# One hybrid trunk layer on one core: the last gate goes to memory in one write by rows, and the writes of the turned residual stand further apart

## The chip, the core and the metric

The kernel runs on one core of a Trainium2 chip. The metric is the device time of one execution in microseconds (us), start to end; lower is better. The core's engines work side by side, each through its own list of instructions in a fixed order: TensorE (PE in the profile; PEld is its loading of weights), VectorE (DVE), ScalarE (ACT), GpSimd (POOL) and SyncE (SP). A DMA is issued by one of them, stands in that engine's list, and is carried out beside it.

## What is computed

One layer over 128 context tokens and 256 latent tokens, 2048 wide, in single precision. Six modulation vectors come from `c` (latent) and `c_ctx` (context). The sixth, `g2`, is the last gate: it weighs the output of the feed-forward part before the residual is added.

```python
m = (jax.nn.silu(cvec) @ w_ada + b_ada)          # adaln: 6 x 2048, for c_ctx and for c
sh1, sc1, g1, sh2, sc2, g2 = split(m, 6)
h = rmsnorm(x, norm_mix) * (1.0 + sc1) + sh1
x = x + g1 * token_mixers(h)                     # w_in, four mixers, w_out
h = rmsnorm(x, norm_ffn) * (1.0 + sc2) + sh2
a = dwconv3(h @ w_up, w_conv)                    # 2048 -> 2 x 5632
val, gate = split(a, 2)
x = x + g2 * ((val * silu(gate)) @ w_down)       # 5632 -> 2048
y = rmsnorm(x, norm_final)
```

## The kernel before

**Tiling.** Until the feed-forward part, activations lie with features on the 128 partitions: `x2` is four tiles of 4 x 384 (four blocks of 128 features, 384 tokens). Every product is done three times, with high and low parts of both factors: each weight chunk of 128 x 1024 (512 KB, tile `raw`) is loaded by SP, cast to `whi` on ACT (line 90 of the profile is the helper that records all DVE and ACT work), and the rest `wlo` is taken on DVE. Chunks are loaded into five `raw` buffers, so SP issues a load when DVE and ACT are done with an older one.

**Feed-forward part.** The 44 blocks of hidden features are cut into three parts of 16, 14 and 14 (`PARTS`). Each part is an up-projection (`up_group`: two blocks at a time, eight chunks of `w_up`, 24 matmuls of 384 tokens per chunk into five rotating accumulators) and then a down-projection (`down_group`: four quarters `q4` of the 2048 outputs, matmuls of 512 columns) whose output has tokens on the partitions. Only the last part's down-projection adds the gate and the residual (`base`, `collect`). For that both must be had with tokens on partitions, and they go through memory:

- `turn` (spawned in the second group of the first part) transposes each `x2[q4]` on DVE in blocks of 32 x 32 into a tile `turn` and writes that to `turned` with 16 DMAs of 32 x 12 x 32 elements, issued by POOL.
- `ada_mod_dve(5, ...)` makes the gate `g2`. Its 32 weight chunks (`w_ada_dve`, through the same `raw` buffers) are mixed among the up-projection's chunks of the first part; DVE multiplies and adds them into two rows `aacc`. After each eighth chunk, that is for each quarter, a `later` sums the partitions with 16 small matmuls (`ps_mod`), transposes on DVE (`tr`), adds the bias into `mods` (features on partitions), and then calls `out`, which writes the quarter's `mods[:, 5]` to `gates` with two DMAs on POOL, one per token group, element by element: 128 x 4 single values each.
- `base(q4)` reads `gates` back, broadcast over the partitions, and `turned`.

**Order.** Nothing is scheduled by the hardware. A planner (`Pipe`) walks the chunks in order, keeps an estimated time `now`, and lets generators ("threads") emit their next piece when their time has come: `yield 12.0` means that the generator continues 12 us of planner time later. The result is one fixed list per engine. At run time an instruction waits only for the one ahead of it on its engine and for data and buffers; a planned pause is no wait.

Of the kernel before, what the change touches and what calls it, by code (L numbers as in the profile page):

```python
# [7 lines left out]
F32 = mybir.dt.float32  # L8
# [6 lines left out]
P = 128  # L15
D = 2048
KD = D // P
# [217 lines left out]
def trunk(ctx, tc, a, o):  # L235
# [6 lines left out]
    tmp = ctx.enter_context(tc.tile_pool(name="tmp", bufs=2))  # L242
# [19 lines left out]
    pipe = Pipe(nc, {"spare": Spare(), "pairs": Pairs(), "raw": WPool(5), "hi": WPool(3), "lo": WPool(3)}, {"raw": 5, "pairs": 4}, 2, 2.5)  # L262
    V, S, G, PE, SY = pipe.V, pipe.S, nc.gpsimd, nc.tensor, nc.sync

    def slot(name, dtype=F32, shape=(P, 4, T)):
        return sp.tile(list(shape), dtype, tag="s", name=name)
# [4 lines left out]
    def wide(name):  # L271
        return hp.tile([P, 512], F32, name=name, tag="v2", bufs=4)
# [10 lines left out]
    def misc(name):  # L283
        return psm.tile([P, 512], F32, tag="m", name=name)
# [24 lines left out]
    ident = misc_c[:, 0:P]  # L309
# [20 lines left out]
    mods = const.tile([P, 6, KD, 2], F32, name="mods")  # L330

    gates = dram.tile([2, D], F32, name="gates")
# [109 lines left out]
    def columns(ps, n, place):  # L442

        tr = tmp.tile([P, 8, 32], F32, name="tr")
        V.transpose(tr[:, 0:n].rearrange("p j c -> p (j c)"), ps[:, 0:32 * n])
        j0 = 0
        for i, k0, m in place:
            dst = mods[:, i, k0:k0 + m]
            V.tensor_add(dst, tr[:, j0:j0 + m, 0:2], b_ada[:, i, k0:k0 + m].unsqueeze(2).to_broadcast([P, m, 2]))
            if i in (1, 4):  # L450
                nm = at["norm_mix" if i == 1 else "norm_ffn"][:, k0:k0 + m]
                V.scalar_tensor_tensor(out=dst, in0=dst, scalar=1.0, in1=nm.unsqueeze(2).to_broadcast([P, m, 2]), op0=ALU.add, op1=ALU.mult)
            j0 += m
# [29 lines left out]
    ada_acc, pending, ada_done = {}, [], {}  # L483

    def ada_dve(src, key, k2, place, then=None):

        def mm(c):
            raw = c["raw"].rearrange("p (k n) -> p k n", k=2)
            if k2 == 0:
                while len(pending) > 1:  # L490
                    pipe.finish(pending.pop(0))
                ada_acc[key] = [wide("aacc0"), wide("aacc1")]
            t = ada_acc[key]
            for kk in range(2):
                k = 2 * k2 + kk
                for v in range(2):
                    if k == 0:
                        V.tensor_scalar(out=t[v], in0=raw[:, kk], scalar1=sv[:, k, v:v + 1], scalar2=None, op0=ALU.mult)
                    else:
                        V.scalar_tensor_tensor(out=t[v], in0=raw[:, kk], scalar=sv[:, k, v:v + 1], in1=t[v], op0=ALU.mult, op1=ALU.add)  # L500
            if k2 == 7:
                def later():
                    ps = misc("ps_mod")
                    for v in range(2):
                        for s in range(4):
                            PE.matmul(ps[32 * s:32 * s + 32, 0:P], pick[:, 31 - v:63 - v], t[v][:, s * P:(s + 1) * P], start=v == 0, stop=v == 1, tile_position=(0, 32 * s))
                    pipe.now += 0.56
                    yield 0.4
                    columns(ps, 4, place)
                    yield  # L510
                    if then:
                        then()
                pending.append(later())
                ada_done[key] = pending[-1]
                pipe.spawn(pending[-1], "d")
            yield 0.0
        return dict(src=src, mm=mm, split=False)

    def ada_mod_dve(i, q4s):
        def out(q4):  # L520
            for v in range(2):
                G.dma_start(gates[v].rearrange("(m p) -> p m", p=P)[:, 4 * q4:4 * q4 + 4], mods[:, i, 4 * q4:4 * q4 + 4, v])
        return [ada_dve(a["w_ada_dve"][i - 2, q4, k2], (i, q4), k2, [(i, 4 * q4, 4)], (lambda q4=q4: out(q4)) if i == 5 else None)
                for q4 in q4s for k2 in range(8)]


# [429 lines left out]
    for g in range(N_WIN):  # L956
        if g == W_CB:
            before = len(last)
        last += win_group(g, 2, evs.get(g) or (lambda zt, m, t, hd=g - W_H0: ev_head(zt, m, t, hd)))
    side_dve = [c for i, q4s in ADA_DVE if i == 2 for c in ada_mod_dve(i, q4s)]  # L960
    side_pe = [c for i, hs in ADA_PE for c in ada_mod_pe(i, hs)]
    side_pe, held = side_pe[:-len(ADA_HELD)], side_pe[-len(ADA_HELD):]
# [150 lines left out]
    def turn():  # L1113

        for q4 in range(4):
            t = slot("turn").rearrange("p k t -> p (k t)")
            V.transpose(t, x2[q4].rearrange("p k t -> p (k t)"))
            yield "d"
            for i in range(4):
                for q in range(4):  # L1120
                    f = (4 * q4 + i) * P + 32 * q
                    G.dma_start(turned.rearrange("(b i) f -> i b f", i=32)[:, :, f:f + 32], t[32 * q:32 * q + 32, i * T:(i + 1) * T].rearrange("p (b j) -> p b j", j=32))
            yield 12.0

    def g_slots(i):
        gh[i] = slot(f"gh{i}", F32R)
# [2 lines left out]
    def up_group(part, i):  # L1129
# [3 lines left out]
        for k2 in range(8):  # L1133
            def pre(k2=k2):
                if k2 == 0 and i == 0:
                    if part == 0:
                        pipe.finish(FF["norm"])
                    gh.clear()
                    gl.clear()
                if k2 == 0 and i % 2 == 0:  # L1140
                    g_slots(i // 2)
                if k2 == 0 and i == 1 and part == 0:
                    pipe.spawn(turn())
                if part == 0 and i == 0:
                    need_h(min(2 * k2 + 4, KD))

            def mm(c, k2=k2):
                if k2 == 0:
                    accs.extend([acc("acc0"), None, acc("acc2"), None])
                    accs[1], accs[3] = acc("acc1"), acc("acc3")  # L1150
                hi = c["hi"].rearrange("p (k n) -> p k n", k=2)
                lo = c["lo"].rearrange("p (k n) -> p k n", k=2)
                for m in (0, 2, 1, 3):
                    w = slice(m * P, (m + 1) * P)
                    for kk in range(2):
                        k = 2 * k2 + kk
                        mm_a(accs[m][:, 0:T], hi[:, kk, w], lo[:, kk, w], hh[k // 4][:, k % 4], hl[k // 4][:, k % 4], k == 0, k == KD - 1)
                        yield 3 * T_MM
                    if k2 == 7 and m >= 2:
                        pipe.start(glu(accs[m - 2][:, 0:T], accs[m][:, 0:T], b0 + m - 2, kb + m - 2))  # L1160
            out.append(dict(src=a["w_up"][b0 // 2, k2], mm=mm, pre=pre))
# [28 lines left out]

    def base(q4):

        pipe.finish(ada_done[5, q4])
        f = slice(512 * q4, 512 * q4 + 512)
        rows[q4], gate[q4] = slot(f"rows{q4}"), slot(f"gate{q4}")
        rows[q4] = rows[q4].rearrange("p k t -> p (k t)").rearrange("p (g f) -> p g f", g=NG)
        gate[q4] = gate[q4].rearrange("p k t -> p (k t)").rearrange("p (g f) -> p g f", g=NG)
        G.dma_start(gate[q4][:, 0:2], gates[:, f].rearrange("(o v) f -> o v f", o=1).to_broadcast([P, 2, 512]))
        G.dma_start(rows[q4], turned[:, f].rearrange("(g p) f -> p g f", p=P))
        G.dma_start(gate[q4][:, 2], a["norm_row"][f].rearrange("(o f) -> o f", o=1).to_broadcast([P, 512]))  # L1200
        yield 9.0
        for g in range(NG):
            V.tensor_mul(sums[q4][:, g], sums[q4][:, g], gate[q4][:, min(g, 1)])
            V.tensor_add(sums[q4][:, g], sums[q4][:, g], rows[q4][:, g])
            yield
# [40 lines left out]
    def down_group(part, q4):  # L1246
# [30 lines left out]
        return out  # L1277

    g2 = [c for i, q4s in ADA_DVE if i == 5 for c in ada_mod_dve(i, q4s)]
    for part, (b0, n) in enumerate(PARTS):  # L1280
        ups = [c for i in range(n // 2) for c in up_group(part, i)]
# [132 lines left out]
```

## Time and profile before

| | |
|---|---|
| median of 3 runs | 1787.3 us |
| the runs | 1788.08, 1778.97, 1787.3 us |
| the profiled execution's own time | 1780.96 us |
| span in its trace (first to last instruction) | 1779.2 us |
| TensorE busy | 1741.4 us, 98% |
| DVE, ACT, POOL busy | 1120.3, 711.3, 72.6 us |
| mean granted TensorE clock | 0.994 of full speed |

The trace counts time from the start of the span; 1.8 us of the profiled execution lie around it. In rows of stretches, PE is the time in which a matmul was under way, with the count of matmuls in brackets, and PEclk the granted clock. The first up-projection runs from about 657 to 945 us, its down-projection follows.

### The profile page before, as it was taken

Reading aid. Unit: us, or ns where it says so; the run is one execution under the profiler, and the core shown is the slowest. Engines: PE = TensorE matmul, PEld = TensorE weight load, DVE = VectorE, ACT = ScalarE, POOL = GpSimd, SP = SyncE. Lnnn points to the kernel's source line nnn. Section 1 sums busy time; section 2 is a strip of 40 time slices with the busy share of each in tenths; the row PEclk is TensorE's granted clock in tenths of the full one; section 3 lists DMA queues with packets and bytes.
Section 4 is the critical chain, followed back from the end, with each engine's and each line's share of the span. In section 5 each row is a group of like instructions: output and inputs, shape, how many; then the busy total and the mean of one; then the engine's idle time right before and its main releaser. Section 6 shows DMA issues by size and latency. Waiting matters only on the chain.

```text
span 1779.2 us, 26710 instructions
## 1 busy us (share of the span) xinstructions
PE 1741.4 (98%) x10704; PEld 1613.7 (91%) x10704; DVE 1120.3 (63%) x1871; ACT 711.3 (40%) x1074; POOL 72.6 (4%) x118
## 2 busy tenths in 40 slices
PE   8999999999999999998999999999999999999998
PEld 6989889989989989997998889999998899999886
DVE  4595678888986578886975333545543344464656
ACT  5523342234643256343433323434432233443433
POOL 0000000000001002500000000000000000000000
PEclk9999999999999999999999999999999999999999
DMA  8878776576645755776677344443443354434642
GB/s 336 283 286 307 278 255 227 184 245 215 218 131 179 294 209 171 244 189 154 204 164 160 127 128 129 130 126 123 131 127 127 125 166 130 125 125 135 221 140 97
DMA packets 93246, 326.69 MB, mean 184 GB/s; under 512 B 11393, under 2 KB 13697, under 8 KB 93121
## 3 DMA queue, kind: packets, MB, share of 16 engines
q1 hardware_dynamic: 86640, 307.78, 53.8%
q0 software_dynamic: 5760, 16.01, 3.0%
q8 instruction: 84, 1.38, 0.3%
q10 hardware_dynamic: 720, 1.18, 0.2%
q14 instruction: 42, 0.34, 0.0%
HBM read 318.10 MB, written 6.83 MB: 183 GB/s over the span
## 4 chain that ended last, share of the span: by engine, by line
PE 61%; DVE 4%; DMA 4%; ACT 1%; issue 1%; POOL 0%; ACTq 0%; DVEq 0%; POOLq 0%
PE acc L530 13%; PE acc L528 13%; PE acc L529 13%; PE acc L535 7%; PE acc L534 7%; PE acc L533 7%; DMA raw<-in_w_up 4%; DVE aacc L90 1%; DVE wlo L90 1%; DVE glu L90 1%; PE ps_sc L287 0%; DMA xr<-in_xT 0%; ACT whi L90 0%; PE ps_ada L468 0%; DVE xr L90 0%
## 5 line engine op out<-in xcount | busy, mean ns | idle before, releaser
L90 DVE TENSOR_TENSOR wlo<-raw,whi 128x1024 fp32r<-128x1024 f32 x384 | 468.8, 1222 | 502.5 <-ACT whi L90 500.4
L90 ACT CAST whi<-raw 128x1024 fp32r<-128x1024 f32 x384 | 402.9, 1050 | 879.7 <-PE acc L529 380.2
L528 PE MATMUL acc<-h2h,whi 128*128 128x384 f32 x1408 | 473.4, 336 | 9.5 <-ACT whi L90 5.7
L530 PE MATMUL acc<-h2h,wlo 128*128 128x384 f32 x1408 | 472.9, 336 | 2.4 <-DVE wlo L90 2.4
L529 PE MATMUL acc<-h2l,whi 128*128 128x384 f32 x1408 | 472.3, 335 | 0.3
L528 PEld LDWEIGHTS acc<-h2h,whi 128*128 128x128 f32 x1408 | 265.8, 189 | 12.5 <-ACT whi L90 6.7
L530 PEld LDWEIGHTS acc<-h2h,wlo 128*128 128x128 f32 x1408 | 265.7, 189 | 4.3 <-DVE wlo L90 4.3
L529 PEld LDWEIGHTS acc<-h2l,whi 128*128 128x128 f32 x1408 | 265.7, 189 | 0.9 <-DVE h2l L90 0.8
L535 PE MATMUL acc<-whi,gl 128*128 128x512 f32 x528 | 205.5, 389 | 0.0
L534 PE MATMUL acc<-wlo,gh 128*128 128x512 f32 x528 | 205.4, 389 | 0.0
L533 PE MATMUL acc<-whi,gh 128*128 128x512 f32 x528 | 205.4, 389 | 0.0
L528 PE MATMUL acc<-hh,whi 128*128 128x384 f32 x576 | 199.2, 346 | 0.9 <-DVE z L90 0.9
L530 PE MATMUL acc<-hh,wlo 128*128 128x384 f32 x576 | 193.2, 336 | 0.8 <-DVE wlo L90 0.8
L529 PE MATMUL acc<-hl,whi 128*128 128x384 f32 x576 | 192.8, 335 | 0.2 <-DVE hl L90 0.2
L90 DVE SCALAR_TENSOR_TENSOR aacc<-raw,svp,aacc 128x512 f32<-128x512 f32 x270 | 184.7, 744 | 0.0
L90 DVE SCALAR_TENSOR_TENSOR glu<-up,sm,glu 128x127 f32<-128x127 f32 (+1 forms) x352 | 135.3, 414 | 26.7 <-ACT glu L90 20.5
L528 PEld LDWEIGHTS acc<-hh,whi 128*128 128x128 f32 x576 | 108.1, 188 | 11.8 <-issue 7.5
L534 PEld LDWEIGHTS acc<-wlo,gh 128*128 128x128 f32 x528 | 99.1, 188 | 20.7
L535 PEld LDWEIGHTS acc<-whi,gl 128*128 128x128 f32 x528 | 99.1, 188 | 20.5
L533 PEld LDWEIGHTS acc<-whi,gh 128*128 128x128 f32 x528 | 99.1, 188 | 20.4
L530 PEld LDWEIGHTS acc<-hh,wlo 128*128 128x128 f32 x576 | 108.1, 188 | 1.5 <-DVE wlo L90 1.5
L529 PEld LDWEIGHTS acc<-hl,whi 128*128 128x128 f32 x576 | 108.2, 188 | 1.0 <-DVE hl L90 0.4
(175 smaller groups left out, 1610.1 us busy)
## 6 DMA issues: line engine op xcount, KB each, us to landing
raw<-in_w_up SPq DMA_DIRECT2D x176, 512.0 KB, 3.6
raw<-in_w_in SPq DMA_DIRECT2D x88, 512.0 KB, 4.8
raw<-in_w_down SPq DMA_DIRECT2D x88, 512.0 KB, 3.5
raw<-in_w_ada SPq DMA_DIRECT2D x64, 512.0 KB, 5.6
raw<-in_w_ada_dve SPq DMA_DIRECT2D x64, 512.0 KB, 4.5
raw<-in_w_ada_pe SPq DMA_DIRECT2D x64, 512.0 KB, 4.9
raw<-in_w_out SPq DMA_DIRECT2D x32, 512.0 KB, 4.3
x<-in_xT SPq DMA_DIRECT2D x4, 768.0 KB, 7.9
```

Of the source, the lines that this page charges most:

```text
L90: return f(*args, **kw)
L528: PE.matmul(out, wh, xh, start=first, stop=False)
L529: PE.matmul(out, wh, xl, start=False, stop=False)
L530: PE.matmul(out, wl, xh, start=False, stop=last)
L533: PE.matmul(out, xh, wh, start=first, stop=False)
L534: PE.matmul(out, xh, wl, start=False, stop=False)
L535: PE.matmul(out, xl, wh, start=False, stop=last)
```

## The change

The write of the gate is made once, after the last quarter, in place of two writes after each. DVE gathers `mods[:, 5]` into `gate_v` (128 x 32, token group by token group), one transpose on TensorE turns it into 32 rows of 128 (`ps_gate`), ACT copies them out of the accumulator memory (`gate_r`), and one DMA on POOL writes 32 runs of 128 elements. `base` no longer waits in the planner for the gate's quarter; that the write has been emitted is asserted. In `turn` the pause now stands inside the loop over the four blocks, after every fourth write, and is 14 in place of 12.

```diff
+    def rows_of_gate():
+        g = tmp.tile([P, 2, KD], F32, name="gate_v", bufs=1)
+        V.tensor_copy(g, mods[:, 5].rearrange("p m v -> p v m"))
+        yield
+        ps = misc("ps_gate")
+        PE.transpose(ps[0:2 * KD, 0:P], g.rearrange("p v m -> p (v m)"), ident)
+        yield 0.3
+        t = tmp.tile([2 * KD, P], F32, name="gate_r", bufs=1)
+        S.copy(t, ps[0:2 * KD, 0:P])
+        G.dma_start(gates.rearrange("v (m p) -> (v m) p", p=P), t)
+        gate_out.append(1)
...
     def ada_mod_dve(i, q4s):
-        def out(q4):
-            for v in range(2):
-                G.dma_start(gates[v].rearrange("(m p) -> p m", p=P)[:, 4 * q4:4 * q4 + 4], mods[:, i, 4 * q4:4 * q4 + 4, v])
-        return [ada_dve(..., (lambda q4=q4: out(q4)) if i == 5 else None)
+        def out():
+            pipe.spawn(rows_of_gate())
+        return [ada_dve(..., out if (i, q4) == (5, 3) else None)
...
                     G.dma_start(turned.rearrange(...)[:, :, f:f + 32], t[32 * q:32 * q + 32, i * T:(i + 1) * T]...)
-            yield 12.0
+                yield 14.0
...
     def base(q4):
-        pipe.finish(ada_done[5, q4])
+        assert gate_out
```

POOL's list from the second normalisation's small power (`n_q`) to the first read of the last part, before:

```order
L385 TENSOR_TENSOR n_q<-n_r,mhalf 128x3
L1122 DMA turned<-turn 32x12x32 x64
L522 DMA gates<-mods 128x4x1 x8
L1198 DMA gate_14632<-gates 128x2x512
L1199 DMA rows_14631<-turned 128x3x512
```

and with the change:

```order
L385 TENSOR_TENSOR n_q<-n_r,mhalf 128x3
L1136 DMA turned<-turn 32x12x32 x60
L529 DMA gates<-gate_r 32x128
L1136 DMA turned<-turn 32x12x32 x4
L1212 DMA gate_14631<-gates 128x2x512
L1213 DMA rows_14630<-turned 128x3x512
```

Eight writes of the gate have become one; it stands ahead of the last four writes of `turned`, and nothing else stands between the writes of `turned`.

DVE's list around the gate's first quarter (`tr` and `mods`; `turn` is the block transpose of one residual tile `xr`), before:

```order
L90 STREAM_TRANSPOSE turn<-xr_5907 128x1536
L90 TENSOR_TENSOR wlo<-raw,whi 128x1024 x2
L90 SCALAR_TENSOR_TENSOR aacc_7000<-raw,svp,aacc_7000 128x512
L90 SCALAR_TENSOR_TENSOR aacc_7001<-raw,svp,aacc_7001 128x512
L90 SCALAR_TENSOR_TENSOR aacc_7000<-raw,svp,aacc_7000 128x512
L90 SCALAR_TENSOR_TENSOR aacc_7001<-raw,svp,aacc_7001 128x512
L90 TENSOR_TENSOR wlo<-raw,whi 128x1024
L90 STREAM_TRANSPOSE tr<-ps_mod 128x128
L90 TENSOR_TENSOR mods<-tr,sm 128x8
L90 TENSOR_TENSOR wlo<-raw,whi 128x1024
```

and with the change:

```order
L90 TENSOR_TENSOR wlo<-raw,whi 128x1024
L90 STREAM_TRANSPOSE tr<-ps_mod 128x128
L90 TENSOR_TENSOR mods<-tr,sm 128x8
L90 STREAM_TRANSPOSE turn<-xr_5166 128x1536
L90 TENSOR_TENSOR wlo<-raw,whi 128x1024
```

Before, the fourth residual tile (`xr_5907`) is turned ahead of the gate's first quarter; now the second one (`xr_5166`) is turned right behind it. Counted in weight splits (`wlo`) from the kernel's start, the four block transposes stood behind the 130th, 134th, 138th and 142nd and now stand behind the 130th, 145th, 160th and 176th; the gate's four quarters stand behind the 145th, 159th, 173rd and 185th in both.

TensorE's list around the new transpose, with the change:

```order
L542 MATMUL acc_8858<-h2h_6713,whi 128x384
L543 MATMUL acc_8858<-h2l_6714,whi 128x384
L544 MATMUL acc_8858<-h2h_6713,wlo 128x384
L542 MATMUL acc_8858<-h2h_6713,whi 128x384
L543 MATMUL acc_8858<-h2l_6714,whi 128x384
L544 MATMUL acc_8858<-h2h_6713,wlo 128x384
L525 MATMUL ps_gate<-misc_c,gate_v 32x128
L542 MATMUL acc_8859<-h2h_6713,whi 128x384
L543 MATMUL acc_8859<-h2l_6714,whi 128x384
```

Six more matmuls of the up-projection stand ahead of these, so twelve in all between the gate's last small products (`ps_mod`) and the transpose (`ps_gate`); before, the same row of matmuls runs on without it.

## Rows read from the trace of the kernel before

**Rows 1.** The page's first part: busy us, share of the span, instructions.

```profile
PE 1741.4 (98%) x10704; PEld 1613.7 (91%) x10704; DVE 1120.3 (63%) x1871; ACT 711.3 (40%) x1074; POOL 72.6 (4%) x118
```

**Rows 2.** Engines by stretches: us; busy (count) of PE, PEld, DVE, ACT, POOL; PEclk; DMA; GB/s.

```profile
692.86:751.00 58.14, 58.14 (x338) 58.14 (x337) 55.40 (x84) 22.30 (x30) 33.48 (x55) 1.00 0.72 224
757.60:776.00 18.40, 17.75 (x100) 16.82 (x99) 14.72 (x28) 5.79 (x9) 1.57 (x3) 1.00 0.86 137
776.00:810.00 34.00, 33.71 (x195) 33.40 (x194) 32.60 (x53) 15.51 (x22) 0.00 (x0) 1.00 0.65 215
812.00:846.00 34.00, 27.04 (x143) 25.76 (x142) 19.60 (x35) 10.11 (x16) 1.54 (x2) 0.90 0.72 139
...
884.00:912.00 28.00, 24.21 (x122) 23.57 (x121) 15.80 (x23) 7.30 (x11) 1.49 (x2) 0.88 0.88 156
912.00:939.00 27.00, 27.00 (x157) 27.00 (x156) 26.44 (x44) 10.46 (x14) 0.00 (x0) 1.00 0.64 214
941.00:960.00 19.00, 19.00 (x91) 16.47 (x91) 13.71 (x25) 10.97 (x17) 1.47 (x2) 1.00 0.89 81
```

**Rows 3.** The chain that ended last, in order of time: start us, us, what.

```profile
760.76 12.40 DMA raw<-in_w_up
...
816.29 17.77 DMA raw<-in_w_up
...
887.28 14.75 DMA raw<-in_w_up
...
939.52 0.57 PE ps_mod L506 x16
```

**Rows 4.** DMA issues of 692 to 757.6, then of 886 to 903: KB, us to landing.

```profile
raw<-in_w_up SPq DMA_DIRECT2D x15, 512.0 KB, 4.9
...
raw<-in_w_up SPq DMA_DIRECT2D x2, 512.0 KB, 14.5
```

**Rows 5.** POOL's instructions in order of time: start us, us, what, idle before.

```profile
692.86 7.37 POOL L1122 DMA_DIRECT2D turned<-turn  x12 [42.38 <-DVE glu L90]
...
757.64 1.52 POOL L522 DMA_DIRECT2D gates<-mods  x2
...
814.44 1.54 POOL L522 DMA_DIRECT2D gates<-mods  x2 [55.27 <-DVE mods L90]
...
886.41 1.49 POOL L522 DMA_DIRECT2D gates<-mods  x2 [70.43 <-DVE mods L90]
...
940.97 1.49 POOL L522 DMA_DIRECT2D gates<-mods  x2 [53.07 <-DVE mods L90]
```

**Rows 6.** DMA issues of the whole span: KB each, median us to landing.

```profile
turned<-turn POOLq DMA_DIRECT2D x64, 48.0 KB, 4.4
...
gates<-mods POOLq DMA_DIRECT2D x8, 2.0 KB, 15.6
```

**Rows 7.** TensorE's matmuls in order of time, behind the second pair of gate writes.

```profile
826.93 0.34 PE L530 MATMUL acc<-h2h,wlo 128*128 128x384 f32 x1
829.86 0.45 PE L528 MATMUL acc<-h2h,whi 128*128 128x384 f32 x1 [2.59 <-ACT whi L90]
...
835.64 0.69 PE L528 MATMUL acc<-h2h,whi 128*128 128x384 f32 x1 [3.56 <-ACT up L90]
836.13 0.52 PE L529 MATMUL acc<-h2l,whi 128*128 128x384 f32 x1
```

**Rows 8.** DVE's instructions in order of time: a block transpose, and the last quarter.

```profile
744.79 1.77 DVE L90 STREAM_TRANSPOSE turn<-xr 128x1536 f32<-128x1536 f32 x1
...
940.51 0.17 DVE L90 TENSOR_TENSOR mods<-tr,sm 128x8 f32<-128x8 f32 x1
942.28 1.22 DVE L90 TENSOR_TENSOR wlo<-raw,whi 128x1024 fp32r<-128x1024 f32 x1 [1.60 <-ACT whi L90]
```

**Rows 9.** Four transposes on TensorE in the mixers, and ACT's copy of their output.

```profile
518.73 0.60 PE L835 MATMUL ps_vt<-misc_c,hw 128*128 128x128 f32 x4
...
519.37 0.59 ACT L90 COPY vT<-ps_vt 128x512 f32<-128x512 f32 x1 [2.70 <-PE ps_vt L835]
```

More of the change, by code (lines that the diff above doesn't have):

```diff
@@ L517, in ada_dve @@
         return dict(src=src, mm=mm, split=False)
+    def rows_of_gate():
[9 more added lines that the diff above has]
+        gate_out.append(1)
+    gate_out = []
     def ada_mod_dve(i, q4s):
-        def out(q4):
-            for v in range(2):
-                G.dma_start(gates[v].rearrange("(m p) -> p m", p=P)[:, 4 * q4:4 * q4 + 4], mods[:, i, 4 * q4:4 * q4 + 4, v])
-        return [ada_dve(a["w_ada_dve"][i - 2, q4, k2], (i, q4), k2, [(i, 4 * q4, 4)], (lambda q4=q4: out(q4)) if i == 5 else None)
+        def out():
+            pipe.spawn(rows_of_gate())
+        return [ada_dve(a["w_ada_dve"][i - 2, q4, k2], (i, q4), k2, [(i, 4 * q4, 4)], out if (i, q4) == (5, 3) else None)
                 for q4 in q4s for k2 in range(8)]
```

## The prediction, made before the changed kernel ran

> **What bounds the kernel now.** I read the page's first part, then the chain of waits in order of time, then engines by stretches around the place that the diff touches, then the transfers there. TensorE is busy 1741.4 of 1779.2 us [rows 1], so only time that it loses can be won. The diff touches the first up-projection, 657 to 945 us. There the chain, elsewhere a string of matmuls, three times passes through a weight load that is far too long: 12.40 us from 760.76, 17.77 from 816.29, 14.75 from 887.28 [rows 3]; over the stretch 692 to 757.6 the same 512 KB take 4.9 us [rows 4]. Each of the three starts 1 to 3 us behind a pair of gate writes on POOL's queue (757.64, 814.44, 886.41; the fourth pair at 940.97) [rows 5]. Such a write carries 2 KB in 512 single elements and takes 15.6 us to land; a write of a turned tile carries 48 KB and takes 4.4 [rows 6]. While a pair is under way the core's traffic falls from 224 GB/s to 137, 139, 156 and 81 [rows 2], and 512 KB loads take 14.5 us in the third such stretch [rows 4]. The fourth pair is the best witness: at 941 the gate's own products on DVE are over and the down-projection runs, yet traffic falls all the same, and TensorE, with loads ready ahead, loses nothing (19.00 busy of 19.00).
>
> What TensorE loses is more than its idle time. At 829.86 it had waited 2.59 us, at 835.64 another 3.56, and it then restarts at the lower of its two clock levels: one matmul takes 0.52 us where one takes 0.34 us otherwise [rows 7]; the granted clock is 0.90 over 812 to 846 and 0.88 over 884 to 912 [rows 2]. So I count matmuls, which takes in both. The undisturbed pace is 58.14 us / 338 = 0.172 us, and 27.00 / 157 = 0.172 again [rows 2].
>
> **What the change removes.** Lost time is stretch minus count times pace [rows 2]; no small products for the gate fall into these stretches:
> 757.6 to 776: 18.40 - 100 x 0.172 = 1.20
> 776 to 810 (the tail of the first): 34.00 - 195 x 0.172 = 0.46
> 812 to 846: 34.00 - 143 x 0.172 = 9.40
> 884 to 912: 28.00 - 122 x 0.172 = 7.02
> 941 to 960: 0.
> Sum 18.1 us, the bound of this part's gain. All 4096 single elements go; one write of 32 rows of 128 elements stands in for them. It issues where the fourth pair did (about 943 us), where even 81 GB/s cost nothing, and its reader comes only in the last down-projection. I price it at 0; its upper end is the 1.2 us of the first pair.
>
> **What it adds.** A copy of 32 columns on DVE: DVE idles 1.60 us between the last gate addition (940.51, 0.17 us) and the next split at 942.28 [rows 8], and a copy of this size costs about what the addition did. The transpose on TensorE is on the path. Four transposes with four times the weight columns took 0.60 us together [rows 9], so one is between 0.15 and 0.60; I take 0.2. It stands 12 matmuls, 2.1 us, behind the gate's products, which end near 940.1 (939.52 + 0.57) [rows 3]; what it waits for is ready near 940.9. That is 1.2 us of slack; if DVE were later than that, every up-matmul behind the transpose would wait as long. The copy out on ACT stands ahead of the accumulators' copies and costs at most 0.59 (a copy of 512 columns) [rows 9]; five accumulator buffers cover it, without them it is on the path.
>
> **What it moves.** The four big transposes on DVE keep their 1.77 us each [rows 8], and so does the first one its place. The next three move by 11, 22 and 34 weight splits: to right behind the gate's addition of the first quarter, one split behind that of the second and three behind that of the third. Their writes follow, and here the diff's longer pause says more than the program does: POOL's queue holds nothing between the 16 writes of one tile, so the pause spaces tiles, not writes. A tile's writes still leave in one burst, as the 12 that went in 7.37 us from 692.86 [rows 5]. Only the last four are apart, behind the gate's write, which waits for ACT; nobody waits for them before the last part. So three bursts come to stand almost where the three harmful gate writes stood. What a burst costs is read from 692.86 to 757.6, where all four ran: through 751 TensorE is busy 58.14 of 58.14 and 224 GB/s flow beside DVE's 55.40 [rows 2]. I take 0 us; the far end is what a harmful pair cost, 9.4 each. DVE has less idle time left when the stalls are gone: it is at 55.40 of 58.14 with four transposes inside and at 26.44 of 27.00 later, without TensorE waiting [rows 2]. I take 0 for that too.
>
> A rule that speaks against the first of these zeros: the Trainium skill, "DMA: Bandwidth & Descriptors", Specifications, wants at least 512 B in one run and has shorter ones handled by read-modify-write. A burst is 16 x 384 runs of 128 B, six times the 1024 elements of a gate pair, so counted by short runs a burst would be the worse of the two, and the sum would be rival A's, 1791, not 1763. The trace does not bear that out: 224 GB/s with bursts, 137 to 156 with gate writes.
>
> The sum: 1780.96 - 18.1 + 0.2 = 1763.1 us for the profiled execution. It is 6.3 under the median; the four known executions lie at 1779, 1781, 1787 and 1788. One trace can't tell where the other 8 us sit. The stalls differ from pair to pair within one run (1.7, 9.4, 7.0, 0), so part of the spread may be theirs and go with them (1763), or it is elsewhere and stays (1769). **I forecast 1765 us.**
>
> **Rivals.**
> A, slower: the bursts take over. They now meet the stretches with the shallowest lead, where weight loads and the gate's own loads share five buffers. If a burst holds loads back as a gate pair does, three cost, at the worst pair's price, 3 x 9.4 = 28.2: 1780.96 - 18.1 + 28.2 = 1791, and 1797 against the median. It decides near 12 us from issue to landing: the load of 12.40 us cost 1.7 in all, those of 17.77 and 14.75 cost 9.4 and 7.0 [rows 3]. Against it: in the stretch with all four bursts loads landed in 4.9 us [rows 4].
> B, part stays: one burst or the fuller DVE queue costs about 9, half of the gain: 1772, or 1778 against the median. For it: DVE at 26.44 of 27.00 [rows 2].
> C, the gate writes are not the cause: the loads of the gate's weights, or the boundary between its quarters, stall the queue, and the time stays 1781 to 1787. Against it: the fourth pair, where those loads are over and 81 GB/s remain, and the undisturbed 912 to 939 where they run at 214 GB/s [rows 2]. By the Trainium skill, "DMA: Bandwidth & Descriptors", Anatomy of one DMA, a transfer costs a constant 2.0 us plus its bytes, and many descriptors can be emitted before it shows; by that rule 2 KB writes would harm nobody and C would hold with no change in time. The trace disagrees, with 15.6 us to landing for 2 KB.
>
> **How the numbers follow.** Forecast 0.73, A 0.05, B 0.14, C 0.08. The measurement tells about 0.5% from no change, which is 8.9 us: faster means under 1778.4, slower over 1796.2. The forecast is faster throughout, B mostly, C and most of A are neither: faster 0.84, same 0.12, slower 0.04. Low end: the fastest run less the sum is 1778.97 - 18.1 = 1760.9, and I allow 4 more for a second spread that goes with the stalls: 1757. High end: B against the median, 1778, which leaves out A and C and a little of B.
>
> **What would show it.** In the new profile: no single-element writes; traffic near 200 GB/s and a granted clock of 1.00 over the whole up-projection up to its end, which comes some 18 us sooner; no wait of the weights' cast for a load beyond 5 us; three bursts of turned writes near 755, 815 and 885 us with TensorE busy beside them; the new transpose without idle time ahead of it. It is wrong if TensorE idles over 1 us behind a burst (A, B), if long loads remain without gate writes (C), or if the transpose waits for DVE.

## The result and the profile after

The changed kernel takes 1762.8 us (median of four runs, 1761.6 to 1763.6), the kernel before 1786.1 in runs beside it (1779.0 to 1788.1). The ratio is 0.9876, 95% interval 0.9847 to 0.9905: faster by 1.2%. The forecast was 1765 within 1757 to 1778. The profiled execution took 1763.55 us with a span of 1761.8, against 1780.96 and 1779.2.

The page's first part, same columns as [rows 1]:

```profile
PE 1734.2 (98%) x10705; PEld 1609.6 (91%) x10705; DVE 1120.8 (64%) x1872; ACT 713.3 (40%) x1075; POOL 67.1 (4%) x111
```

TensorE does one instruction more (the transpose) and is busy 7.2 us less, though its work has not shrunk: fewer of its matmuls ran at the lower clock. The other 10 us of the gain are idle time.

Engines by stretches, kernel after; the first six lines are the stretches of [rows 2] up to 912 us (846 to 882 has been added), the last one holds the new end of the up-projection:

```profile
692.86:751.00 58.14, 58.14 (x337) 58.14 (x336) 52.65 (x84) 23.66 (x32) 9.88 (x16) 1.00 0.65 204
757.60:776.00 18.40, 18.40 (x108) 18.40 (x107) 17.89 (x34) 8.14 (x13) 8.02 (x14) 1.00 0.72 211
776.00:810.00 34.00, 33.97 (x203) 33.54 (x201) 30.65 (x50) 15.54 (x22) 0.00 (x0) 1.00 0.63 201
812.00:846.00 34.00, 34.00 (x198) 34.00 (x197) 31.47 (x51) 14.15 (x20) 9.72 (x16) 1.00 0.75 233
846.00:882.00 36.00, 36.00 (x221) 35.55 (x220) 31.80 (x52) 14.84 (x21) 0.00 (x0) 1.00 0.64 203
884.00:912.00 28.00, 28.00 (x163) 28.00 (x163) 27.25 (x44) 12.78 (x19) 7.30 (x12) 1.00 0.65 203
924.00:942.00 18.00, 18.00 (x87) 15.46 (x86) 13.14 (x25) 10.73 (x18) 2.96 (x5) 1.00 0.47 143
```

Read four columns. PE is busy throughout. From 757 to 846 us 509 matmuls run in the three stretches where 438 ran (8 of the 509 are small products of the gate, which stood outside these stretches before), and 163 in 884 to 912 where 122 ran. The granted clock is 1.00 everywhere (it was 0.90 and 0.88). The traffic stays between 203 and 233 GB/s in the stretches that fell to 137, 139 and 156. POOL's count shows where the turned tiles' writes now are: 14, 16 and 12 of them in just these stretches.

What ACT's cast of the weights waited for, from 690 us to the end of the gate's quarters (in total, times, longest). Before:

```profile
ACT whi L90 <- DMA raw<-in_w_up: 97.5, 26, 13.0
```

After:

```profile
ACT whi L90 <- DMA raw<-in_w_up: 45.4, 18, 4.7
```

The long waits are gone (longest 4.7 in place of 13.0 us). The chain that ended last goes through one load of the up-projection's weights, of normal length, where [rows 3] had three of 12 to 18 us. The after kernel's chain in order of time (start, us, what) begins the stage with the first line and ends it with the third:

```profile
658.51 0.44 PE acc L543
...
805.52 3.62 DMA raw<-in_w_up
...
921.94 0.57 PE ps_mod L506 x16
```

The same first matmul in the chain of before:

```profile
657.25 0.45 PE acc L529
```

From the first up-matmul to the gate's last small products it takes 939.52 - 657.25 = 282.27 us before [rows 3] and 921.94 - 658.51 = 263.43 after: 18.8 less. Ahead of it the after kernel happens to be 1.26 us later, in code that the change leaves alone. Behind it 1779.2 - 939.52 = 839.7 us before and 1761.8 - 921.94 = 839.9 after, 0.2 more. So the whole gain of the span, 17.4 us, is in this stage.

### The profile page after: what moved, and what is told of

Same layout as the page of the kernel before. It is cut to its first block, busy times and chain, and to the rows that moved or that the text cites. A ratio compares the mean times of both kernels' runs of the same rounds, so it can differ in the third digit from the quotient of the medians.

```text
span 1761.8 us, 26700 instructions
## 1 busy us (share of the span) xinstructions
PE 1734.2 (98%) x10705; PEld 1609.6 (91%) x10705; DVE 1120.8 (64%) x1872; ACT 713.3 (40%) x1075; POOL 67.1 (4%) x111
## 4 chain that ended last, share of the span: by engine, by line
PE 68%; DVE 2%; DMA 1%; ACT 0%; issue 0%; POOL 0%; DVEq 0%; POOLq 0%
PE acc L542 15%; PE acc L544 15%; PE acc L543 15%; PE acc L549 7%; PE acc L547 7%; PE acc L548 7%; DMA xr<-in_xT 0%; PE ps_sc L287 0%; PE ps_ada L468 0%; DVE glu L90 0%; DVE aacc L90 0%; DVE wlo L90 0%; DVE xr L90 0%; DMA raw<-in_w_up 0%; PE ps_bc L287 0%
```

## The experiments

Each kernel was timed beside the kernel before on the same chip. In the three sets of runs, the kernel before had medians of 1791.4, 1783.8 and 1794.0 us, so each ratio goes by its own neighbour. The times that were expected were set by the 1786 us of the first runs; on the slower chips the kernels that keep the price can come out above them, as the kernel before does.

### Which part of the change is it?

The write of the gate alone: the after kernel with the old pause, which puts the turned tiles' writes back to their early place.

```diff
-                yield 14.0
+            yield 12.0
```

> The changed kernel with the old pause: one write of the gate by rows, the turned tiles' writes bunched between 692 and 758 us as before. Theory (the single-element writes alone held the loads back; the pause brings nothing): 1763 us, ratio to before 0.987, TensorE not idle through the whole up-projection, and within 2 us of the changed kernel. Rival (the pause is part of the gain, since the first gate pair met the fourth tile's burst): 1765 us or more, with the lost time behind 757 us. Rival (another cause at the gate's quarters): 1786 us.

Measured 1762.2 us (1761.5 to 1763.0), ratio 0.984 [0.9818, 0.9862]. Two stretches of it:

```profile
692.00:757.00 65.00, 65.00 (x389) 64.56 (x388) 59.62 (x90) 25.76 (x36) 38.10 (x63) 1.00 0.74 231
757.60:776.00 18.40, 18.40 (x108) 18.40 (x107) 18.15 (x34) 7.87 (x12) 0.39 (x1) 1.00 0.62 179
```

63 of the 64 turned writes stand in 65 us again, beside a TensorE that is busy in all of them, and none stands in the next two stalls' places. The gain is whole without the pause.

The pause alone, in the kernel before:

```diff
-            yield 12.0
+                yield 14.0
```

> The kernel before with the new pause alone: four gate pairs of single elements stay, three bursts of turned writes now stand right behind them on POOL's queue. Theory: none of the gain, 1783 to 1788 us; a burst behind a gate pair waits in POOL's list or adds a little, so up to 1792. Rival (the pause gives part of the gain): under 1780 us. Three long loads of 12 us and more remain behind the gate pairs in the theory.

Measured 1793.6 us (1790.0 to 1796.8), ratio 1.0014 [0.9996, 1.0031]. Its chain in order of time holds the three long loads as before:

```profile
758.31 18.87 DMA raw<-in_w_up
...
825.57 19.36 DMA raw<-in_w_up
...
898.43 17.88 DMA raw<-in_w_up
```

So the pause is worth nothing, and the gate's write is the whole change.

### What about the gate's write is dear?

The after kernel differs from before in the number of writes, their place in time, and their form. The next kernels keep number and place (two writes behind each quarter, on POOL) and alter the form alone. The first writes runs of four elements (16 B), contiguous on both sides; the gate then lies in memory in another order, and the last part reads it as if it lay in the old one. So this kernel and the next four (all up to the one with fewer single elements) compute another output; their times show what the writes cost beside the same loads and the same matmuls.

```diff
-                G.dma_start(gates[v].rearrange("(m p) -> p m", p=P)[:, 4 * q4:4 * q4 + 4], mods[:, i, 4 * q4:4 * q4 + 4, v])
+                d = gates.rearrange("v f -> (v f)").rearrange("(q p m v) -> p q m v", p=P, q=4, v=2)[:, q4]
+                G.dma_start(d[:, 2 * v:2 * v + 2].rearrange("p m v -> p (m v)"), mods[:, i, 4 * q4 + 2 * v:4 * q4 + 2 * v + 2].rearrange("p m v -> p (m v)"))
```

> The kernel before with its eight gate writes in their places and of the same 2 KB each, but as 128 runs of 16 bytes in place of 512 of 4 (the gate's values land in another order in memory, which the last part then reads so). Theory (the price goes by the number of runs): a pair is under way about 4 us in place of 13 to 16, no load lasts over 9 us, TensorE loses under 2 us in all, 1763 to 1766 us. Rival (the price goes by the write, its place or its bytes): 1786 us, with the same three long loads.

Measured 1763.0 us (1762.7 to 1763.2), ratio 0.9844 [0.9822, 0.9866]: all of the gain, with the same 2 KB per write, the same issuer and the same places behind the quarters. DMA issues (count, KB each, median us to landing):

```profile
gates<-mods POOLq DMA_DIRECT2D x8, 2.0 KB, 3.8
```

The second puts the four elements of a partition side by side in memory, where they stood 512 B apart. A whole write fills one piece of 2 KB there in both kernels; only the order within it changes. In `mods` the four stay every second element, so each is still a run of its own on that side.

```diff
-                G.dma_start(gates[v].rearrange("(m p) -> p m", p=P)[:, 4 * q4:4 * q4 + 4], mods[:, i, 4 * q4:4 * q4 + 4, v])
+                G.dma_start(gates[v].rearrange("(q p m) -> p q m", p=P, q=4)[:, q4], mods[:, i, 4 * q4:4 * q4 + 4, v])
```

> The kernel before with its eight gate writes as single elements still, 512 of them each, but landing side by side in memory (runs of four neighbours, each written on its own, in another order than the last part expects) in place of 512 bytes apart. Theory (the number of runs counts, not where they land): the stalls stay, 1783 to 1788 us, gate writes land after 12 to 17 us. Rival (scattered targets in memory are the price): the writes land within 6 us and the time is 1763 to 1770 us.

Measured 1798.4 us (1795.3 to 1803.3), ratio 1.0042 [1.0023, 1.006]: no better, rather a little worse. Its writes:

```profile
gates<-mods POOLq DMA_DIRECT2D x8, 2.0 KB, 17.0
```

The two kernels write to neighbouring places alike; they differ in whether a partition's four elements are read as one run or as four. But a write of runs also has a quarter of the runs. So the next one has 512 runs of 16 B in each write, as many as there were single elements, by sending each partition's run four times (the line removed is the same as above, here and in the next two):

```diff
+                d = gates.rearrange("v f -> (v f)").rearrange("(h j p e) -> h p j e", h=2, j=4, p=P)[v]
+                G.dma_start(d, mods[:, i, 4 * q4 + 2 * v:4 * q4 + 2 * v + 2].rearrange("p m v -> p (m v)").unsqueeze(1).to_broadcast([P, 4, 4]))
```

> The kernel before with its eight gate writes in their places, each as 512 runs again, but of 16 bytes (each value is written four times to different places, 8 KB a write; the last part reads a gate in another order). Theory 1 (the number of runs sets the price): the stalls are back, 1783 to 1797 us, landing 12 us and more. Theory 2 (the single element sets it): no long load, 1762 to 1767 us, landing under 9 us. Runs of 16 bytes, a quarter as many, took 4.6 us to land and cost nothing.

Measured 1763.1 us (1761.6 to 1763.9), ratio 0.9883 [0.9854, 0.9913]. Its writes:

```profile
gates<-mods POOLq DMA_DIRECT2D x8, 8.0 KB, 5.0
```

(The 4.6 us that the expectation gives for the runs of four is a median that takes in the reads of the gate; the writes alone landed in 3.8.) The number of runs is not the price. Then 512 runs of two elements (8 B), each write carrying the whole quarter, 4 KB:

```diff
+                d = gates.rearrange("v f -> (v f)").rearrange("(q h j p e) -> q h p j e", q=2, h=2, j=4, p=P)[q4 // 2, v]
+                G.dma_start(d, mods[:, i, 4 * q4:4 * q4 + 4])
```

> The kernel before with its eight gate writes in their places, each as 512 runs of 8 bytes, 4 KB a write (both token groups' values side by side, written in two places; the last part reads a gate in another order). Theory 1 (only the single element of 4 bytes is dear, as 512 runs of 16 bytes cost nothing): 1762 to 1767 us, landing under 9 us. Theory 2 (the price grows steadily as the run gets shorter): a pair is under way 7 us and more, one or two loads over 10 us, 1766 to 1780 us.

Measured 1764.2 us (1763.6 to 1766.0), ratio 0.9838 [0.982, 0.9856]. Its writes:

```profile
gates<-mods POOLq DMA_DIRECT2D x8, 4.0 KB, 6.6
```

Of the lengths that the gate was written in here (4, 8, 16 and, in the after kernel, 512 B), only single elements of 4 B cost anything. Do fewer of them cost less? Here two writes of 128 runs of 16 B carry the quarter, and two more bring 128 single elements each, a quarter of what there was:

```diff
+                d = gates.rearrange("v f -> (v f)").rearrange("(q p m v) -> p q m v", p=P, q=4, v=2)[:, q4]
+                G.dma_start(d[:, 2 * v:2 * v + 2].rearrange("p m v -> p (m v)"), mods[:, i, 4 * q4 + 2 * v:4 * q4 + 2 * v + 2].rearrange("p m v -> p (m v)"))
+            for v in range(2):
+                G.dma_start(gates[v].rearrange("(m p) -> p m", p=P)[:, 4 * q4:4 * q4 + 1], mods[:, i, 4 * q4:4 * q4 + 1, v])
```

> The kernel before where at each quarter two writes of 128 runs of 16 bytes (free by themselves) are followed by two writes of 128 single elements, a quarter of the single elements of before (the last part reads a gate that is partly in another order). Theory (each single element has its price): a pair holds the loads back 3 to 5 us, which TensorE's lead covers, 1762 to 1766 us. Rival (any write by single elements holds the loads back for a fixed time): long loads over 12 us and 1778 us or more.

Measured 1794.3 us (1791.1 to 1798.5), ratio 1.0006 [0.9994, 1.0017]: the price is not halved, it is all there. Its writes of runs and its writes of single elements:

```profile
gates<-mods POOLq DMA_DIRECT2D x8, 2.0 KB, 3.8
...
gates<-mods POOLq DMA_DIRECT2D x8, 0.5 KB, 15.2
```

512 bytes in 128 single elements take 15.2 us to land and hold the loads as long (20.37, 17.49 and 11.15 us in the chain) as 2 KB in 512 of them did. So within these sizes it is not a price per element either. Per write, then? This kernel sends each single-element write a second time, into a second tensor:

```diff
                 G.dma_start(gates[v].rearrange("(m p) -> p m", p=P)[:, 4 * q4:4 * q4 + 4], mods[:, i, 4 * q4:4 * q4 + 4, v])
+                G.dma_start(gates2[v].rearrange("(m p) -> p m", p=P)[:, 4 * q4:4 * q4 + 4], mods[:, i, 4 * q4:4 * q4 + 4, v])
```

> The kernel before with each of the eight gate writes made twice, the second into another tensor, so 2048 single elements at each of the four places. Theory (each single element has its price, and TensorE pays what its lead does not cover): each place holds the loads back for some 13 us more, all of which TensorE pays at the first three, and part at the fourth: 39 to 52 us more than the kernel before, ratio 1.02 to 1.03. Rival (a fixed price per place): ratio 1.00.

Measured 1834.2 us (1830.7 to 1840.4), ratio 1.023 [1.0202, 1.0259], 40 us more than the kernel before on that chip. Its writes:

```profile
gates<-mods POOLq DMA_DIRECT2D x16, 2.0 KB, 30.1
```

and its chain in order of time:

```profile
763.09 27.87 DMA raw<-in_w_up
...
835.95 32.40 DMA raw<-in_w_up
...
921.57 21.49 DMA raw<-in_w_up
...
991.14 29.98 DMA raw<-in_w_down
```

Twice as many writes at one place take twice as long to land (the trace holds a landing for 2 of the 16 only, each the last of its four), and the three long loads of the up-projection take 27.87, 32.40 and 21.49 us where [rows 3] had 12.40, 17.77 and 14.75. Against the kernel with runs of 8 B on the same chip (1764.2), the kernel before loses 29.8 us and this one 70.0: more than twice, which fits a lead that covers the first part of each hold only. The fourth place, free before, now stands in the chain too.

### Who issues it, and where?

The same single-element writes from ACT's queue:

```diff
-                G.dma_start(gates[v].rearrange("(m p) -> p m", p=P)[:, 4 * q4:4 * q4 + 4], mods[:, i, 4 * q4:4 * q4 + 4, v])
+                S.dma_start(gates[v].rearrange("(m p) -> p m", p=P)[:, 4 * q4:4 * q4 + 4], mods[:, i, 4 * q4:4 * q4 + 4, v])
```

> The kernel before with the same eight single-element writes issued from ACT's queue in place of POOL's. Theory (what holds the loads back is the elements, whoever issues them): three long loads as before, 1780 to 1797 us. Rival (it is POOL's queue, which carries the turned tiles too): 1762 to 1768 us.

Measured 1787.8 us (1780.9 to 1791.6), ratio 1.0021 [1.0002, 1.0041]. Its writes:

```profile
gates<-mods ACTq DMA_DIRECT2D x8, 2.0 KB, 14.0
```

The long loads stay (17.14, 18.36 and 15.67 us in its chain). It is not POOL's way of issuing. Nor is it the number of packets into which a write is split. The trace counts packets by queue (packets, MB, share of the time of the 16 DMA engines). One pair of writes from ACT's queue, 895 to 913 us:

```profile
q10 hardware_dynamic: 1056, 0.00, 3.3%
```

One pair from POOL's queue, in the kernel before (814 to 833 us) and in the kernel with runs of four (813 to 832 us):

```profile
q0 software_dynamic: 64, 0.00, 1.1%
...
q0 software_dynamic: 64, 0.00, 0.3%
```

The loads are held beside 1056 packets and beside 64, and they are not held beside 64 packets that carry runs of 16 B.

The next was to move all eight single-element writes behind the last quarter:

```diff
-        def out(q4):
-            for v in range(2):
+        def out():
+            for q4 in range(4):
+                for v in range(2):
...
-        return [ada_dve(a["w_ada_dve"][i - 2, q4, k2], (i, q4), k2, [(i, 4 * q4, 4)], (lambda q4=q4: out(q4)) if i == 5 else None)
+        return [ada_dve(a["w_ada_dve"][i - 2, q4, k2], (i, q4), k2, [(i, 4 * q4, 4)], out if (i, q4) == (5, 3) else None)
...
-        pipe.finish(ada_done[5, q4])
+        pipe.finish(ada_done[5, 3])
```

> The kernel before with all eight single-element writes behind the gate's last quarter, where the down-projection has begun and one pair cost nothing in the trace of before. Theory (a pair cost nothing there because TensorE had some 12 us of loads ahead, not because the place is immune): four pairs hold the loads back for 50 us and more, and TensorE loses 10 to 30 us there, 1773 to 1793 us. Rival (the place is immune, as long as the gate's own loads are over): 1763 us, no idle time.

Measured 1784.3 us (1780.9 to 1788.6), ratio 0.9999 [0.9982, 1.0016]. It did not test its question. POOL's instructions in order of time:

```profile
817.80 1.55 POOL L523 DMA_DIRECT2D gates<-mods  x2 [57.90 <-DVE mods L90]
```

A write that is later in the program, on a queue that holds nothing else, still leaves when its own data are there: at 758, 818, 889 and 944 us as before. The repeat therefore copies the gate once on DVE behind the last quarter and writes from the copy (the other lines change as above):

```diff
+        def out():
+            g = tmp.tile([P, KD, 2], F32, name="gate_c", bufs=1)
+            V.tensor_copy(g, mods[:, 5])
+            for q4 in range(4):
+                for v in range(2):
+                    G.dma_start(gates[v].rearrange("(m p) -> p m", p=P)[:, 4 * q4:4 * q4 + 4], g[:, 4 * q4:4 * q4 + 4, v])
...
```

> The kernel before with all eight single-element writes taken from a copy that DVE makes behind the gate's last quarter, so that they can only leave there, near 925 us, where the down-projection begins. Theory (a pair cost nothing there because TensorE had loads ahead, not because the place is immune): four pairs in a row hold the loads back for 50 us and more, TensorE loses 10 to 30 us behind 925 us and nothing ahead of it, 1773 to 1793 us. Rival (the place is immune once the gate's own loads are over): 1763 us.

Measured 1771.8 us (1769.3 to 1773.5), ratio 0.9882 [0.986, 0.9904]: 7.6 us above the kernel with runs of 8 B on the same chip, a little less than expected at the least. The place is not free, but it is cheaper than the old ones. All eight leave from 923.16 us on. Its writes:

```profile
gates<-gate_c POOLq DMA_DIRECT2D x8, 2.0 KB, 31.3
```

a load in its chain:

```profile
932.53 27.41 DMA raw<-in_w_down
```

and its stretches behind them (columns as in [rows 2]):

```profile
923.00:933.00 10.00, 10.00 (x51) 9.00 (x50) 7.42 (x16) 7.93 (x13) 5.98 (x8) 1.00 0.40 60
933.00:943.00 10.00, 10.00 (x46) 8.27 (x45) 5.24 (x9) 3.03 (x4) 0.00 (x0) 1.00 0.51 29
943.00:953.00 10.00, 9.09 (x41) 7.22 (x39) 1.34 (x2) 1.04 (x2) 0.00 (x0) 1.00 1.11 71
953.00:963.00 10.00, 7.27 (x22) 5.05 (x23) 2.34 (x2) 1.18 (x2) 0.00 (x0) 0.83 0.79 154
```

The core's traffic stays at 29 to 71 GB/s for 30 us, and yet TensorE is busy on work that it has ready until past 950. Only then does it idle, and come back at a lower granted clock (0.83). The traffic is hardly lower than behind the fourth pair of before, only low for longer; before:

```profile
943.00:953.00 10.00, 10.00 (x49) 8.67 (x48) 8.61 (x20) 6.92 (x12) 0.00 (x0) 1.00 1.02 34
```

In their four old places the same eight writes cost 29.8 us on this chip, four times as much. That eight in a row land in 31 us (median of the five landings that the trace holds; the last comes 36.5 us after the first issue), about as four do in the kernel that writes twice, says that the price is not a fixed one per write, as far as two places with different loads beside them can be compared.

### Can the bursts of turned writes cost anything?

Each turned write doubled, in the after kernel:

```diff
                     G.dma_start(turned.rearrange("(b i) f -> i b f", i=32)[:, :, f:f + 32], t[32 * q:32 * q + 32, i * T:(i + 1) * T].rearrange("p (b j) -> p b j", j=32))
+                    G.dma_start(turned.rearrange("(b i) f -> i b f", i=32)[:, :, f:f + 32], t[32 * q:32 * q + 32, i * T:(i + 1) * T].rearrange("p (b j) -> p b j", j=32))
```

> The changed kernel with every write of a turned tile made twice, 128 in place of 64, so each burst is 32 writes and about 20 us long. Theory (bursts of 128-byte runs cost nothing where they now stand): within 2 us of the changed kernel, 1761 to 1765 us. Rival A of the prediction, in its mild form (a burst eats TensorE's lead): 1768 us or more, with idle time of TensorE behind 755, 820 or 886 us.

Measured 1762.4 us (1762.1 to 1766.0), ratio 0.9886 [0.985, 0.9923] against before, beside the after kernel's 1762.8 us no change. One of its stretches:

```profile
812.00:846.00 34.00, 34.00 (x198) 34.00 (x197) 31.49 (x51) 14.13 (x20) 8.72 (x15) 1.00 0.71 225
```

It is a weaker test than was meant. The second write of a place waits for the first, so the writes ran in a steady row, a pair every 3 to 5 us from 693 past 970 us, instead of in longer bursts. What it shows is that 128 such writes, all along the up-projection, cost nothing measurable.

## Why the prediction was right, step by step

**What bounds it.** Right. Loads held up behind the gate's writes were the lost time; without the single elements (the after kernel and five experiments) TensorE is busy in all but 0.2 us of any of the stretches there (33.83 of 34.00 at the least); in the after kernel the loads of this stage land in 3.8 us.

**The removed part, 18.1 us.** Measured 18.8 in the stage. Counting matmuls by the undisturbed pace took in idle time and lowered clock together, and that is why it came close: PE's busy time alone fell by 7.2 us, its idle time by the other 10. The remaining 0.7 us is a little in each term. The up-projection's matmuls stand in the same order in both kernels, so the start of one and the same matmul can be compared:

| the same matmul starts at (us) | before | after | after is ahead by |
|---|---|---|---|
| ahead of the first stall | 757.63 | 758.89 | -1.26 |
| behind it | 781.15 | 780.39 | 0.76 |
| behind the second | 850.09 | 839.70 | 10.39 |
| behind the third | 912.14 | 894.56 | 17.58 |

The stalls cost 2.0, 9.6 and 7.2 us where the sum had 1.7, 9.4 and 7.0.

**The transpose, 0.2 us.** Right: behind the stage the span is 0.2 us longer. TensorE's matmuls around it, in order of time:

```profile
924.46 0.33 PE L544 MATMUL acc<-h2h,wlo 128*128 128x384 f32 x1
924.63 0.27 PE L525 MATMUL ps_gate<-misc_c,gate_v 128*32 128x128 f32 x1
924.66 0.43 PE L542 MATMUL acc<-h2h,whi 128*128 128x384 f32 x1
```

No idle time stands ahead of it. Its input on DVE, the last gate addition and the new copy in the idle time behind it:

```profile
922.93 0.17 DVE L90 TENSOR_TENSOR mods<-tr,sm 128x8 f32<-128x8 f32 x1
923.13 0.18 DVE L90 COPY gate_v<-mods 128x32 f32<-128x32 f32 x1
924.70 1.23 DVE L90 TENSOR_TENSOR wlo<-raw,whi 128x1024 fp32r<-128x1024 f32 x1 [1.39 <-ACT whi L90]
```

The copy is done at 923.31, 1.3 us before TensorE comes to the transpose (1.2 were forecast). ACT's copy out takes 0.26 us where up to 0.59 was allowed:

```profile
924.94 0.26 ACT L90 COPY gate_r<-ps_gate 32x128 f32<-32x128 f32 x1 [0.27 <-PE ps_gate L525]
```

**The one write at 0.** Right: it lands in 1.7 us. The DMA issues of the after kernel:

```profile
turned<-turn POOLq DMA_DIRECT2D x64, 48.0 KB, 3.8
...
gates<-gate_r POOLq DMA_DIRECT2D x1, 16.0 KB, 1.7
```

**The moved bursts at 0, and the pause that spaces tiles, not writes.** Right. POOL's instructions in order of time, kernel after:

```profile
694.12 9.88 POOL L1136 DMA_DIRECT2D turned<-turn  x16 [42.37 <-DVE glu L90]
...
818.62 9.72 POOL L1136 DMA_DIRECT2D turned<-turn  x16 [52.47 <-DVE turn L90]
885.69 6.08 POOL L1136 DMA_DIRECT2D turned<-turn  x10 [57.35 <-DVE turn L90]
...
925.48 0.53 POOL L529 DMA_DIRECT2D gates<-gate_r  x1 [32.27 <-ACT gate_r L90]
926.00 2.45 POOL L1136 DMA_DIRECT2D turned<-turn  x4
```

They leave in bursts of 16, near the places forecast (the second near 756 us), and TensorE stays busy beside each. Rival A falls with it, and with it the reading that short runs as such are harmful: 16 x 384 runs of 128 B per burst cost nothing whether spread or bunched (1762.8 and 1762.2 us). The Trainium skill, "DMA: Bandwidth & Descriptors", Specifications, gives 512 B as the least transfer for full rate, with read-modify-write below it. That did not show as time here for runs of 128, 16 or 8 B.

**DVE's fuller queue at 0.** Right, and with little to spare: DVE is busy 27.25 of the 28.00 us from 884, and 27.71 in the kernel with runs of four, with TensorE never idle. Rival B falls.

**Rival C** falls by the kernels with runs of 8 and 16 B, which keep all loads of the gate's weights, all boundaries between quarters, and two writes at each place, and lose all the stalls. "Anatomy of one DMA" on the same page of the Trainium skill gives a transfer about 2.0 us and its bytes. The write by rows is near that (1.7 us), the runs of 16 B take about twice as long (3.8), and 0.5 KB of single elements does not fit it at all (15.2).

**What was described wrongly.** The prediction put the price on "512 single elements", as if it went by their number, and compared bursts and gate writes by counting runs. 512 runs of 8 or 16 B are free, and 128 single elements cost what 512 do. The cause named was right, its measure was not; the sum did not depend on it.

**The median.** Of the two readings, that the spread of the runs belongs to the stalls (1763) or not (1769), the first was right. The kernel before spread over 1777.7 to 1797.7 in the 48 runs beside the experiments, 8 to 12 us on each of three chips and the rest from chip to chip. The six kernels without single elements stay within 1761.5 to 1766.0, five of them on those same chips. The median gained 23.3 us, 5 more than the sum, which was read from one trace of a faster execution. I took 1765, between the two readings, which is 2 us too much.

**The fourth pair.** That it costs nothing because TensorE has loads ready ahead, and not because the place is immune, is borne out: with twice the writes there, its load of 29.98 us enters the chain, and with all eight there TensorE works on for over 20 us, then idles, and 7.6 us are lost.

**Open.** Why a write of single elements holds up the loads beside it was not shown, nor what its length goes by: two at a place take about 15 us, four 30, eight in a row 31, at 128 or 512 elements each. What the trace does show is where the time sits. The load queue of the kernel before, from 814 to 833 us behind the second pair, and undisturbed from 912 to 939 us (packets, MB, share of the time of the 16 DMA engines):

```profile
q1 hardware_dynamic: 448, 1.64, 78.8%
...
q1 hardware_dynamic: 1586, 5.77, 64.1%
```

A packet of the loads is under way 0.788 x 16 x 19 us / 448 = 0.53 us behind the pair, and 0.17 us undisturbed. So the loads have been issued and lie in the DMA engines, which count as busy with them, while the gate's own packets take 1.1%: by this count it is not they that fill the engines. Single elements from a contiguous source, and ones laid far apart in memory, were not tried.

## What to carry to other kernels

A small result with a stride should be turned on chip and written by rows, or at least in runs of two elements: here that brought 1.2% for one transpose of 0.2 us. A DMA that takes far longer to land than its bytes ask for is to be suspected even where nobody waits for it: look at the landing times of the other loads and at the traffic while it runs. And a write that is put later in the program leaves no later if its queue is empty and its data are there.

## What the runs showed of the hardware that was not expected

- Single elements of 4 B held up the weight loads beside them, while runs of 8 B in the same number were free: 1764.2 against 1794.0 us for the kernel before on that chip.
- The hold does not go by the number of elements: 128 and 512 in a write landed in 15.2 and 15.6 us.
- Laying a partition's four elements side by side in memory did not help while they stood apart in `mods` (1798.4 us, ratio 1.0042).
- Nor did the hold go by the packets of the write: 64 for a pair from POOL's queue, with dear and with free runs alike, and 1056 from ACT's.
- The packets of the loads were under way three times as long meanwhile (0.53 us in place of 0.17 on average).
- Issuing such a write from ACT's queue in place of POOL's did not help (14.0 and 15.6 us to landing; ratio 1.0021).
- With eight of them at one place the core's traffic fell to 29 GB/s over 10 us, and with one pair to 34.
